# Hybrid encoder layer on one core: the first input pieces of the convolution in x landing tiles, the residual of the first tokens later, the gates of half the tokens in one store

## The chip, the cores and the metric

The kernel runs on one core of one Trainium2 chip. The metric is the device time of one execution in microseconds (us). Engines are named as the profile names them: PE (TensorE), ACT (ScalarE), DVE (VectorE), POOL (GpSimd), SP (SyncE, which issues most of the transfers); "L173" is line 173 of the kernel.

## What is computed

One encoder layer on 2048 tokens of 1024 channels, in float32. Cut to its steps:

```python
u = rms_norm(h); proj = u @ w_in
hy = short_conv_centred(proj[..., :HY_COLS])              # z, g1, g2: 512 channels each
for o, gate in enumerate((g1, g2)):                       # hyena: long convolution by rfft of 2L
    conv = irfft(rfft(z, n=2 * L) * spec[:, o], n=2 * L)[:, :L]
    z = gate * (conv + z * skip[o])
y_ml = mlstm_bidirectional(silu(short_conv(q, k)), v, o_pre, gates)   # 16 gate columns a token
h = h + concat(group_norm(z), group_norm(y_ml)) @ w_out
h = h + cross_attention(rms_norm(h), rms_norm(mem))
h = h + square(relu(rms_norm(h) @ ff_w1)) @ ff_w2
return rms_norm(h)
```

`spec` is the spectrum of two-sided filters that a small sine network makes.

## The kernel before

Every large product runs as three matmuls of split operands (high by high, low by high, high by low: L357, L360, L361 in `mm3`). All stages are Python generators that yield a cost; `weave` runs two of them side by side by these costs, so a larger `yield` puts a step later against its partner. The order that comes out is then settled by a scheduler when the program is built; `behind(ins)` (L363) tells it to place an instruction after the matmul issued last, without a semaphore.

**Input projection and filters.** `sweep` (from L749) makes channel blocks of the projection for 1024 tokens at a time, 24 matmuls for a half block of 512 tokens; DVE and ACT convolve the result (L797 to L804), and SP stores it to DRAM (`hy`, `qt`, `kt`). Woven in is `filters` (L232), which makes the filters and their transform by blocks of 32 rows against the constant `f1` (L305 to L311) and stores `fs`. Its tiles lie in the pool `f_sb` (`filters_open`, L341), which closes when it is done.

**Hyena.** `hyena` (L903) is woven with the remaining projection (`weave(rest, p.hyena(hs), 445, 329)`). Its pool `h_sb` takes the space that `f_sb` leaves. It loads `f1` again and `e2`, and then works by steps:
- `load1(j2)` (L934) loads a piece of z from `hy` with four transfers of 128 KB, in a tile of the ring "a" (ten tiles); two pieces are loaded ahead.
- `spectrum(o, j2, z)` (L990) multiplies a piece by `f1` (eight small matmuls through `beside`, L173 and L186), copies the four banks out with ACT and DVE (L997) and stores `zs`. The loop at L1004 does this for eight pieces, with a cost of 3.5 each.
- the loop at L1017 loads blocks of `fs` and `zs` (`load_block`, L915), transforms them (L955 for the filter, L1029 for z), multiplies, transforms back (L986) and stores `zg`. The first L1029 needs pieces of all eight spectra.
- the loop at L1040 loads `zg` and a gate from `hy` (`load3`), multiplies by `e2` (L173 again) and by the gate (L1050). For the first convolution each result goes into `spectrum(1, ...)`, for the second it is normed and stored as `yh`.

**Gates.** `natural` (L861) makes the token-major part of the projection; of its last column block, 16 columns are the gates of a tile of 128 tokens. They go to `sg` (two tiles in turn, L899) and to DRAM with a store per tile (L901). `gates` (L1075) reads them all and scans them on DVE (L1113, L1114).

**mLSTM and attention.** After hyena come `memproj` (L709, L738, keys and values of the memory), with steps of `mlstm` (L1283, L1199, L1321, L1323) set between them. `attention` (L1437) first turns rows of `yh` and `ym` for w_out (L1478), with casts on ACT and DVE at L368; `residual(h)` (L1505) loads half of the 512 tokens' slice of x (1 MB) into `acc`, and `finish` (L1511) adds the product to it.

The transfers of SP are issued in its program order: one whose data is not ready holds up all behind it.

## Time and profile before

| | us |
|---|---|
| median of 3 runs | 3098.77 (3090.32 to 3103.11) |
| the profiled execution | 3100.22 |
| its span in the profile | 3098.5 |
| mean granted clock of PE | 0.984 |

The span is cut in 40 slices by the page; each digit is a busy share in tenths (9 is 90% or more), the last row the mean busy share of the 16 DMA engines:

```profile
PE   9999899999999898999999999999999999999998
DVE  8855365547745445877664666557555686566695
ACT  6443356534744235565544465556555543333335
PEclk9999999999999999999999999999999999999999
DMA  6555578586767996465476556657544565354434
```

A slice is 77 us. The part that the change touches begins in the second (at 149 us, from where two loads of x move away) and ends in the sixteenth; hyena's first matmul stands at 362.67 us and its last wait of PE at 1087.53. In the timelines below, a row gives its start, its length, engine, line, operation, out<-in, and in brackets how long the engine stood idle before it and what ended that. In the rows of stretches: the window, its length, the busy time of PE with the number of instructions, the granted clock, the DMA share and GB/s.

### The profile page before, as it was taken

The page shows a single profiled execution, that of the slowest core. Times are in us where ns is not written, and L with a number is a line of the kernel's source. Part 1 is how long each engine was busy: PE and PEld are TensorE (multiplying, and loading weights), DVE is VectorE, ACT ScalarE, POOL GpSimd, SP SyncE. Part 2 cuts the span into 40 slices and gives each one's busy share as a digit, 9 for nine tenths or more (in the row PEclk, how much of TensorE's full clock was granted, in tenths as well). Part 3 has the DMA queues.
Part 4 walks back from the last instruction along what each step waited for, and adds up shares of the span by engine and source line. Part 5 has one row for each costly group of instructions (what it writes and reads, how often), then busy time and mean ns, then how long its engine had stood idle before and what let it go on. Part 6 is the DMA issues. An engine that isn't in the chain of part 4 may idle for free.

```text
span 3098.5 us, 44022 instructions
## 1 busy us (share of the span) xinstructions
PE 2989.6 (96%) x14799; PEld 2371.5 (77%) x14799; DVE 1945.6 (63%) x3442; ACT 1494.4 (48%) x2930; POOL 1121.0 (36%) x798
## 2 busy tenths in 40 slices
PE   9999899999999898999999999999999999999998
PEld 7666566776577676888888888888888888888876
DVE  8855365547745445877664666557555686566695
ACT  6443356534744235565544465556555543333335
POOL 0111012200222333333132336766466375344653
PEclk9999999999999999999999999999999999999999
DMA  6555578586767996465476556657544565354434
GB/s 223 188 191 175 198 238 250 181 268 201 241 212 217 315 303 195 152 200 167 150 245 217 188 185 226 209 179 241 196 153 151 179 213 175 110 165 119 155 102 163
DMA packets 444618, 607.06 MB, mean 196 GB/s; under 512 B 39262, under 2 KB 249054, under 8 KB 443368
## 3 DMA queue, kind: packets, MB, share of 16 engines
q1 hardware_dynamic: 407012, 546.46, 55.0%
q10 hardware_dynamic: 37380, 57.79, 5.5%
q8 instruction: 117, 1.92, 0.3%
q14 instruction: 109, 0.89, 0.1%
HBM read 401.70 MB, written 202.41 MB: 195 GB/s over the span
## 4 chain that ended last, share of the span: by engine, by line
PE 81%; DMA 9%; DVE 6%; issue 2%; ACT 1%; SPq 1%; POOL 0%; ACTq 0%; DVEq 0%; POOLq 0%
PE mm L357 17%; PE mm L361 17%; PE mm L360 17%; PE hy L357 6%; PE hy L361 6%; PE hy L360 6%; PE hy L173 2%; PE hy L1029 2%; PE hy L986 2%; PE mm L955 2%; DMA a<-zg 1%; PE mm L709 1%; PE hy L1321 1%; DMA xt<-in_x_t_dram 1%; PE hy L1323 1%
## 5 line engine op out<-in xcount | busy, mean ns | idle before, releaser
L1689 ACT CAST ah<-w 128x512 fp32r<-128x512 f32 x284 | 176.6, 623 | 302.1 <-PE hy L360 157.0
L1690 DVE TENSOR_TENSOR bl<-wr,bh 128x512 fp32r<-128x512 f32 x213 | 240.8, 1135 | 126.5 <-ACT bh L1689 126.4
L368 DVE TENSOR_TENSOR wl<-wn,wh 128x512 fp32r<-128x512 f32 (+1 forms) x296 | 215.7, 773 | 101.2 <-ACT wh L368 101.2
L357 PE MATMUL mm<-xh,wh 128*128 128x512 f32 x640 | 267.2, 419 | 3.2 <-ACT st L201 1.4
L360 PE MATMUL mm<-xl,wh 128*128 128x512 f32 x640 | 258.0, 403 | 4.5 <-DVE xl L368 4.4
L1034 POOL TENSOR_TENSOR b<-b,a 128x512 f32<-128x512 f32 x64 | 87.1, 1362 | 481.4 <-ACT b L1032 240.1
L361 PE MATMUL mm<-xh,wl 128*128 128x512 f32 x640 | 257.6, 403 | 0.0
L1689 ACT CAST bh<-wr 128x512 fp32r<-128x512 f32 x232 | 143.6, 621 | 229.9 <-PE mm L361 171.3
L1690 DVE TENSOR_TENSOR al<-w,ah 128x512 fp32r<-128x512 f32 x236 | 214.6, 910 | 55.1 <-ACT ah L1689 55.1
L361 PE MATMUL mm<-bh,al 128*128 128x512 f32 x576 | 224.1, 392 | 4.1 <-DVE al L1690 4.1
L357 PE MATMUL mm<-bh,ah 128*128 128x512 f32 x576 | 226.2, 393 | 0.5 <-DVE acc L1851 0.4
L360 PE MATMUL mm<-bl,ah 128*128 128x512 f32 x576 | 225.1, 391 | 0.0
L368 ACT CAST wh<-wn 128x512 fp32r<-128x512 f32 (+1 forms) x296 | 164.7, 620 | 105.4 <-PE mm L361 50.1
L360 PE MATMUL mm<-act,wh 128*128 128x512 f32 x512 | 201.9, 394 | 0.0
L357 PE MATMUL mm<-act,wh 128*128 128x512 f32 x512 | 199.4, 396 | 1.0 <-ACT wh L368 0.9
L361 PE MATMUL mm<-act,wl 128*128 128x512 f32 x512 | 199.6, 392 | 0.0
L357 PE MATMUL hy<-bh,ah 128*128 128x512 f32 x448 | 175.2, 391 | 0.0
L360 PE MATMUL hy<-bl,ah 128*128 128x512 f32 x448 | 174.6, 390 | 0.0
L361 PE MATMUL hy<-bh,al 128*128 128x512 f32 x448 | 174.4, 390 | 0.0
L357 PEld LDWEIGHTS mm<-xh,wh 128*128 128x128 f32 x640 | 122.4, 191 | 58.2 <-issue 24.3
L360 PEld LDWEIGHTS mm<-xl,wh 128*128 128x128 f32 x640 | 122.8, 192 | 47.4 <-issue 16.3
L357 PE MATMUL mm<-wh,xh 128*128 128x256 f32 (+1 forms) x512 | 157.4, 307 | 0.5 <-ACT st L894 0.5
(380 smaller groups left out, 8077.8 us busy)
## 6 DMA issues: line engine op xcount, KB each, us to landing
wr<-hc SPq DMA_DIRECT2D x224, 256.0 KB
w<-in_ff_w_dram SPq DMA_DIRECT2D x172, 256.0 KB
hc<-wn SPq DMA_DIRECT2D x128, 256.0 KB
wn<-in_w_in_dram SPq DMA_DIRECT2D x100, 256.0 KB
hc<-q SPq DMA_DIRECT2D x96, 256.0 KB
fs<-a SPq DMA_DIRECT2D x32, 512.0 KB
a<-fs SPq DMA_DIRECT2D x64, 256.0 KB
a<-zs SPq DMA_DIRECT2D x64, 256.0 KB
```

Source lines behind the costliest of these rows:

```text
L173: b = self.nc.tensor.matmul(*products[-1], start=True, stop=True)
L357: first = mm(ps, lh, rh, start=start, stop=False)
L360: mm(ps, lh, rl, start=False, stop=False)
L361: self.last = mm(ps, ll, rh, start=False, stop=stop)
L368: both = (self.nc.scalar.copy(hi, src), self.nc.vector.tensor_tensor(lo, src, hi.bitcast(F32), ALU.subtract))
L709: mul(p[:, m], w[:, k, ms], mt[k // 4][:, k % 4], start=k == 0, stop=k == 7)
L955: nc.tensor.matmul(pp, dm[:, m], t[:, m], start=True, stop=True)
L986: nc.tensor.matmul(pg, em[:, m], y, start=True, stop=True)
L1029: nc.tensor.matmul(pp, dm[:, m], t[:, m], start=True, stop=True)
L1034: nc.gpsimd.tensor_tensor(xt, xt, hi[:, m], ALU.mult)
L1689: self.nc.scalar.copy(hi, src)
L1690: eng.tensor_tensor(lo, src, hi.bitcast(F32), ALU.subtract)
```

## The change

Five edits:
- `f1` is one tile of the pool `i_sb`, loaded once in `filters` and used by hyena too; hyena's own load of it is gone.
- pieces 0 and 1 of `load1` go to the two tiles "xn" of `i_sb` (landing tiles of x) instead of the ring "a", which lies in space that the filters still use.
- the cost of a step of the loop over spectra is 4.2 instead of 3.5.
- the gates of eight token tiles are gathered in one tile `sg` (128 x 8 x 16), and one transfer stores them; there is one such tile.
- the load of `residual` for the first 512 tokens is placed behind the matmul issued last.

```diff
--- before.py
+++ after.py
@@ -234,7 +234,7 @@
         sd = [self.dram(f"fs{o}", (16, 64, 4, CH)) for o in range(2)]
         sb, ta, tb = self.fsb, self.ta, self.tb
         if True:
-            fw, hid, f1 = self.f_w, self.f_hid, self.f_f1
+            fw, hid, f1 = self.f_w, self.f_hid, self.f1
             nc.sync.dma_start(out=fw, in_=a["fw"])
             w1, w2, w3 = fw[0:66, 0:128], fw[:, 128:256], fw[:, 256:1280].rearrange("p (o c) -> p o c", o=2)
             par = self.par[:, 128:132]
@@ -341,10 +341,8 @@
     def filters_open(self):
         self.fes = ExitStack()
         self.fsb = self.fes.enter_context(self.tc.tile_pool(name="f_sb", bufs=1))
-        self.fsb.tile([128, 32], F32, name="f_even")
         self.f_w = self.fsb.tile([128, 1280], F32, name="fw")
         self.f_hid = self.fsb.tile([128, 16, 128], F32, name="hid")
-        self.f_f1 = self.fsb.tile([128, 128], F32, name="f1")[:, 0:64]
 
     def ta(self):
         return self.fsb.tile([128, 2, CH], F32, tag="a", name="a", bufs=7)
@@ -446,6 +444,7 @@
         self.xl = xp.tile([128, 8, 1024], F32R, name="xl")
         xp.tile([128, 56], F32, name="x_even")
         small = sb.tile([128, 448], F32, name="small")
+        self.f1 = sb.tile([128, 64], F32, name="f1")
         self.carry = small[:, 0:340].rearrange("p (c t) -> p c t", c=20)
         self.rx, self.rm = small[:, 340:356], small[:, 356:358]
         win = a["w_in"][0]
@@ -896,9 +895,12 @@
                     dst = (self.d_vd if c2 < 2 else self.d_od)[r0 - 128:r0 + 128, 256 * (c2 % 2):256 * (c2 % 2) + 256]
                     nc.scalar.dma_start(out=dst.rearrange("(t p) c -> p t c", p=128), in_=st)
                 if c2 == 3:
-                    sg = sb.tile([128, 16], F32, tag="sg", name="sg", bufs=2)
-                    nc.vector.tensor_tensor(sg, p[:, 256:272], self.gb, ALU.add)
-                    nc.sync.dma_start(out=self.d_gt[r0:r0 + 128], in_=sg)
+                    if t == 0:
+                        sg = sb.tile([128, 8, 16], F32, tag="sg", name="sg", bufs=1)
+                    nc.vector.tensor_tensor(sg[:, t], p[:, 256:272], self.gb, ALU.add)
+                    if t == 7:
+                        dst = self.d_gt[1024 * hf:1024 * hf + 1024]
+                        nc.sync.dma_start(out=dst.rearrange("(t p) g -> p t g", p=128), in_=sg)
 
     def hyena(self, es):
         nc, tc, a = self.nc, self.tc, self.a
@@ -926,13 +928,12 @@
         def tb():
             return sb.tile([128, CH], F32, tag="b", name="b", bufs=5)
 
-        f1 = sb.tile([128, 128], F32, name="f1")[:, 0:64]
+        f1 = self.f1
         e2 = sb.tile([128, 64], F32, name="e2")[:, 0:32]
-        nc.sync.dma_start(out=f1, in_=a["c_f1"])
         nc.sync.dma_start(out=e2, in_=a["c_e2"])
         ghy = self.bcast(sb, a["hy_norm_g"], CH, "ghy")
         def load1(j2):
-            z = ta()
+            z = ta() if j2 > 1 else self.isb.tile([128, D], F32, tag="xn", name="z", bufs=2).rearrange("p (j c) -> p j c", j=2)
             js = slice(2 * j2, 2 * j2 + 2)
             for q in range(4):
                 nc.sync.dma_start(out=z[phase[q]], in_=hy[0, q, :, js])
@@ -1002,7 +1003,7 @@
         yield 52
         self.strict = True
         for j2 in range(8):
-            yield 3.5
+            yield 4.2
             if j2 < 6:
                 q.append(load1(j2 + 2))
             else:
@@ -1504,7 +1505,9 @@
 
             def residual(h):
                 src = a["x_t"].rearrange("(k p) t -> p k t", p=128)[:, 4 * h:4 * h + 4, 512 * c:512 * c + 512]
-                nc.sync.dma_start(out=acc[:, 4 * h:4 * h + 4], in_=src)
+                d = nc.sync.dma_start(out=acc[:, 4 * h:4 * h + 4], in_=src)
+                if c == 0:
+                    self.behind(d)
 
             ssum = A.tile([128, 512], F32, tag="ssum", name="ssum", bufs=2)
```

What stands where, three places. First, SP near the end of the filters, before (`z` and `a<-hy` are pieces of z; `fs` and `zs` the stored transforms; `wn` weights; `f` is f1, `e` is e2; `x12` is twelve transfers):

```order
L829 DMA hy<-st 126x4x128 x2
L838 DMA qt<-cv 128x1008
L339 DMA fs_392<-a 128x1024 x2
L397 DMA wn<-in_w_in_dram 128x2x256 x4
L931 DMA f_2744<-in_c_f_dram 128x64
L932 DMA e_2745<-in_c_e_dram 128x32
L938 DMA a<-hy 32x1024 x12
L838 DMA qt<-cv 128x1008
L943 DMA dm<-in_c_dm_dram 128x256 x2
```

and now, in two stretches, the one where the first pieces stand,

```order
L828 DMA hy<-st 128x4x128 x2
L834 DMA hy<-st 16x128
L939 DMA z<-hy 32x1024 x8
L292 DMA a<-in_c_win_dram 128x1024
L339 DMA fs_390<-a 128x1024 x2
```

and the one at the end of the filters:

```order
L837 DMA qt<-cv 128x1008
L339 DMA fs_391<-a 128x1024 x2
L395 DMA wn<-in_w_in_dram 128x2x256 x4
L933 DMA e_2743<-in_c_e_dram 128x32
L939 DMA a<-hy 32x1024 x4
L944 DMA dm<-in_c_dm_dram 128x256 x2
L939 DMA a<-hy 32x1024 x3
L339 DMA zs_2736<-a 128x1024
L939 DMA a<-hy 32x1024
```

Eight of the twelve transfers moved some 35 rows up, to 213 us of the trace before, right behind the stores of what they read; the load of f1 is gone. In the same place, ACT around the first spectrum's copies (L997, now L998), before:

```order
L311 COPY a<-hy 128x512 x4
L368 CAST wh<-wn 128x512 x4
L789 COPY P<-mm 128x512
L797 ACTIVATE cv<-P,par 128x1008
L379 DMA ghy<-in_hy_norm_g_dram 128x512
L802 ACTIVATE cv<-cv 128x1008
L997 COPY a<-hy 128x512 x2
L339 DMA zs_2737<-a 128x1024
```

and now:

```order
L311 COPY a<-hy 128x512 x4
L366 CAST wh<-wn 128x512 x4
L788 COPY P<-mm 128x512
L796 ACTIVATE cv<-P,par 128x1008
L377 DMA ghy<-in_hy_norm_g_dram 128x512
L998 COPY a<-hy 128x512
L801 ACTIVATE cv<-cv 128x1008
L998 COPY a<-hy 128x512
L339 DMA zs_2736<-a 128x1024
```

One of the two copies now stands ahead of the activation of cv, and the other behind it. Second, SP ahead of the first L1029, before (`kt` is a store of convolved keys, `fs` the filter's blocks):

```order
L339 DMA zs_2737<-a 128x1024
L918 DMA a<-fs_391 128x1x512 x2
L339 DMA zs_2737<-a 128x1024 x2
L918 DMA a<-zs_2737 128x1x512 x2
L918 DMA a<-fs_391 128x1x512 x2
L918 DMA a<-zs_2737 128x1x512 x2
L838 DMA kt<-cv 128x1008
L397 DMA wn<-in_w_in_dram 128x2x256 x3
```

and now:

```order
L339 DMA zs_2736<-a 128x1024
L920 DMA a<-fs_390 128x1x512 x2
L339 DMA zs_2736<-a 128x1024
L837 DMA kt<-cv 128x1008
L395 DMA wn<-in_w_in_dram 128x2x256 x4
L339 DMA zs_2736<-a 128x1024
L837 DMA kt<-cv 128x1008
L920 DMA a<-zs_2736 128x1x512 x2
```

The loads of zs stood right behind the last two stores of zs; now two stores of kt and four loads of weights stand ahead of them too, the first store and the weights between the last two stores of zs. On PE, the fifth and the sixth spectrum stood next to each other, and 24 matmuls stand between them now; between the last spectrum and the first L1029 there were 48 matmuls and four L955, and now there are 23 and four L846. Third, SP at the start of attention, before (`acc` is the residual, `va`, `kn`, `og`, `qn`, `kk_t` and `cbn` belong to steps of mlstm):

```order
L1177 DMA kn<-kn 128x512
L1177 DMA og<-od 128x512
L1258 DMA qn<-qt 128x4x128
L1258 DMA kk_t<-kt 128x4x128
L1507 DMA acc<-in_x_t_dram 128x4x512 x2
L1258 DMA cbn<-cbd 128x516
L1183 DMA va<-vd 128x4x128
L1177 DMA kn<-kn 128x512
```

and now:

```order
L1358 DMA ym<-ht 128x512 x2
L1473 DMA wn<-ym 128x512 x2
L1184 DMA va<-vd 128x4x128
L1259 DMA cbn<-cbd 128x516
L1508 DMA acc<-in_x_t_dram 128x4x512 x2
L1178 DMA kn<-kn 128x512
L1178 DMA og<-od 128x512
L1405 DMA wn<-in_w_out_dram 128x2x256 x4
```

The two loads of the residual stood ahead of the last va; they stand behind it now, and behind the loads of the rows ym.

## The prediction

> **What bounds the kernel now.** I read the page first, then the waits of TensorE (PE), then the stretches in which they lie.

> ```profile
> span 3098.5 us, 44022 instructions
> PE 2989.6 (96%) x14799; PEld 2371.5 (77%) x14799; DVE 1945.6 (63%) x3442; ACT 1494.4 (48%) x2930; POOL 1121.0 (36%) x798
> ```

> PE is busy for 2989.6 of 3098.5 us, and the change leaves its products as they are. So a gain can only come out of the 109 us in which PE stands, and out of the slow clock that follows such a stand. The waits of PE that touch the change (us in total, times, longest):

> ```profile
> PE hy L173 <- DMA a<-hy: 11.7, 1, 11.7
> PE hy L1478 <- DVE act L368: 9.1, 1, 9.1
> PE hy L1029 <- DMA a<-zs: 7.5, 3, 4.0
> ```

> The first two are single stalls. Next, stretches of PE: window, length, busy time, granted clock, DMA share, GB/s.

> ```profile
> 755.00:975.00 220.00, 210.03 (x986) 0.99 0.67 203
> 975.00:1138.00 163.00, 146.68 (x838) 0.96 0.99 316
> 1138.00:1230.00 92.00, 80.72 (x425) 0.93 0.67 221
> ...
> 362.67:368.20 5.53, 5.53 (x25) 0.50 0.97 282
> 396.93:402.00 5.07, 5.07 (x23) 0.50 1.03 324
> 479.00:482.00 3.00, 3.00 (x8) 0.68 0.75 259
> 679.96:685.70 5.74, 5.74 (x25) 0.50 0.88 207
> 919.20:925.00 5.80, 5.73 (x27) 1.00 0.46 128
> 1202.19:1208.00 5.81, 5.80 (x24) 0.50 0.52 156
> ```

> The first three are stages; in the second the DMA engines are full (0.99). The others begin where a stall of PE ends: after the four that begin at 362.67, 396.93, 679.96 and 1202.19, PE ran 5.1 to 5.8 us at clock 0.50, so each such stall costs 2.5 to 2.9 us more than its own length.

> **The change part by part.** The order of PE is the same up to the first spectrum (PE at 351.0 in this trace) and again from about 1225 on, so all terms lie between. "Order us" below is the place of an instruction in the program, counted with these two rows, 24 matmuls of a sweep apart: 5.43 us.

> ```profile
> 415.41 0.79 PE L357 MATMUL mm<-xh,wh 128*128 128x512 f32 x1
> ...
> 420.84 0.39 PE L360 MATMUL mm<-xl,wh 128*128 128x512 f32 x1
> ```

> *1. The first pieces, issued early.* SyncE (SP) before, at two places, and what PE waited for:

> ```profile
> 213.86 0.35 SPq L292 DMA_DIRECT2D a<-in_c_win_dram  x1
> 221.27 1.30 SPq L339 DMA_DIRECT2D fs<-a  x2
> ...
> 355.64 0.34 SPq L931 DMA_DIRECT2D f<-in_c_f_dram  x1
> 356.32 0.34 SPq L932 DMA_DIRECT2D e<-in_c_e_dram  x1
> 356.72 7.84 SPq L938 DMA_DIRECT2D a<-hy  x12
> ```

> ```profile
> 362.67 1.08 PE L173 MATMUL hy<-a,f 32*64 32x512 f32 x1 [11.69 <-DMA a<-hy]
> ```

> Eight of the twelve loads now stand ahead of the c_win load at 213.86. The first spectrum has its data and its constants long before 351.0: -11.69, and -2.8 for the half of 5.53 us at half clock, so **-14.5**. The eight issues take 8 x 0.65 (7.84 / 12) = 5.2 us of SP; behind them stands the c_win load, and SP was idle for 7 us there, up to 221.27, so I take 0 (bounds 0 and +4, if the wait for the stored z comes on top). The f1 load that falls away saves 0.34 us of SP.

> What is late next? The third piece: four loads behind the wn loads, 355.64 + 0.34 + 4 x 0.65 = 358.6 at their end. Before, the first piece's four loads were out by 359.3 and let PE start at 362.67, 3.4 later; so it lands at about 362.0, needed two spectra after 351.0, at 364.0 or later. **0** (bounds 0 and +3; 1 MB of x_t now comes on SP just behind it).

> *2. The second spectrum.* It needs the banks of the first emptied. ACT empties two of them by L997, and the second of these copies now stands behind L802:

> ```profile
> 358.48 1.04 ACT L802 ACTIVATE cv<-cv 128x1008 f32<-128x1008 f32 x1 [2.64 <-DVE cv L800]
> ...
> 364.76 1.08 ACT L997 COPY a<-hy 128x512 f32<-128x512 f32 x2 [5.25 <-PE hy L186]
> ```

> So it ends at 358.48 + 1.04 + 0.54 = 360.1, and PE is there at 351.0 + 1.05 + 5.45 = 357.5: +2.6. Does a stall that short cost clock? The rows go both ways:

> ```profile
> 476.67 1.27 PE L986 MATMUL hy<-b,em 128*128 128x512 f32 x2 [2.06 <-DVE b L1035]
> ...
> 919.27 1.12 PE L986 MATMUL hy<-b,em 128*128 128x512 f32 x2 [2.44 <-DVE b L1035]
> ```

> After 2.06 idle the clock was 0.68 (row 479), after 2.44 it stayed 1.00 (row 919.20). I take half of the 2.6 us of a full spell, +1.3: **+3.9** (bounds 0 and +5.2). [...]

> *3. More sweep between spectra (yield 4.2).* Before, two spectra stood back to back, and the next waited for the copies:

> ```profile
> 396.93 1.11 PE L173 MATMUL hy<-a,f 32*64 32x512 f32 x1 [3.70 <-ACT a L997]
> ```

> Now 24 matmuls (5.43 us) stand between them: -3.70 and -2.5 of clock, **-6.2**. The price is at the other end. From the last spectrum to the first L1029, which needs its result stored and loaded again, there were 14.1 order us; now there are 6.7. How long that path is:

> ```profile
> 412.95 0.64 PE L173 MATMUL hy<-a,f 32*64 32x512 f32 x1
> ...
> 737.29 1.08 PE L173 MATMUL hy<-a,f 32*64 32x512 f32 x1 [3.89 <-issue]
> ...
> 749.15 2.39 PE L1029 MATMUL hy<-a,dm 128*128 128x512 f32 x4 [2.15 <-DMA a<-zs]
> ```

> ```profile
> 419.23 1.17 SPq L918 DMA_DIRECT2D a<-zs  x2
> ```

> At the second convolution it took 749.15 - 737.29 = 11.9 us, waited for, a good 1 us of that by half clock. At the first the loads were out at 420.4, 7.5 after the spectrum at 412.95, and landed within some 3.4: 10.9. I take 10.7 - 6.7 = 4.0 of stall and 2.5 of clock: **+6.5** (bounds 0 and 8.1). A second path gives as much: the a<-zs loads now stand on SP behind stores kt<-cv, which wait for DVE to finish a convolved half.

> For the second convolution the last two spectra now stand 2.1 apart instead of 6.0, and 7.4 order us remain before L1029 (4.5 before, with other stalls between). Against 10.7 that is 3.3 of stall where 2.15 stood: **0** (bounds -2 and +4).

> *4. Gates stored by half.*

> ```profile
> 677.21 0.17 DVE L900 TENSOR_TENSOR sg<-mm,par 128x16 f32<-128x16 f32 x1 [3.74 <-DMA gt<-sg]
> ...
> 679.96 1.11 PE L173 MATMUL hy<-a,f 32*64 32x512 f32 x1 [4.62 <-DVE a L1050]
> ```

> With two sg tiles, DVE stood 3.74 us until a store had landed, and L1050, behind it on DVE, held PE. Eight tokens' tiles now go into one buffer, whose next use is a half later, so nothing waits: -4.62 and -2.9 of clock, **-7.5**. The same bytes go out in 2 transfers for 16. But the gate scan (L1113 and L1114 on DVE), on which the stall at 737.29 above rests, has 13.4 order us of cover between L1092 and L1133 instead of 16.0: **+1.6** of the 2.6 (bounds 0 and +5).

> *5. Residual later, and a denser end of this part.*

> ```profile
> 1190.51 0.92 SPq L1507 DMA_DIRECT2D acc<-in_x_t_dram  x2
> 1192.02 0.74 SPq L1183 DMA_DIRECT2D va<-vd  x1
> ```

> ```profile
> 1230.21 0.69 DVE L1513 TENSOR_TENSOR acc<-mm,acc 128x512 f32<-128x512 f32 x1 [1.14 <-PE mm L361]
> ```

> ```profile
> 1199.66 1.28 ACT L1193 ACTIVATE ve<-va,cols 128x129 f32<-128x129 f32 x4 [4.23 <-DMA va<-vd]
> ```

> ```profile
> 1202.19 1.11 PE L1478 MATMUL hy<-ident,wn 128*128 128x128 f32 x4 [9.05 <-DVE act L368]
> ```

> The 2 MB of acc (6.3 us at 316 GB/s) go ahead of the va load; ACT waits for va at L1193, and its casts for L1478 stand behind. Now acc is issued after va, and DVE wants it only at L1513, 1230.21. So -9.05 and -2.9 go. But hyena ends 32 order us later, so the mLSTM steps before L1478 stand closer, two of them with none of the products L738 between. Such a step:

> ```profile
> 1180.59 1.06 PE L1199 MATMUL hy<-ve,kn 128*128 128x129 f32 x8
> ...
> 1189.05 1.23 PE L1199 MATMUL hy<-ve,kn 128*128 128x129 f32 x8 [0.36 <-ACT ht L1335]
> ```

> It took 8.46 us with L738 in it; bare it has 2.6 order us. Two bare ones stand for between 0 and 2 x 5.9 us; I take 6.2, the middle, and 3.2 of clock: -12.0 + 9.4 = **-2.6** (bounds -12 and +6).

> **Sum:** -14.5 + 0 + 3.9 - 6.2 + 6.5 + 0 - 7.5 + 1.6 - 2.6 = -18.8 us. The profiled execution took 3100.2 us (its span and 1.7 around it), 1.4 over the median of the three runs, 3098.8. So 3081.4 against the profile and 3080.0 against the median; I say **3081**.

> **The rivals.** Half a per cent, 15.5 us, is about what a measurement of this kernel can tell from no change.

> *The waits only move.* The stalls of terms 2, 3 and 5 come at their upper ends (5.2, 8.1 and +6, and 2 more at the second convolution): -14.5 + 5.2 - 6.2 + 8.1 + 2 - 7.5 + 1.6 + 6 = -5.3, so 3095. For it: each place where I put a new stall had little cover. Against it: all at once is much.

> *No new waits.* The prices of terms 2 and 3 vanish and the mLSTM steps cost a quarter: -14.5 - 6.2 - 7.5 + 1.6 - 12.0 + 4 = -34.6, so 3065. Against it: ACT's L802 and the 6.7 us of cover are in the order.

> *The early loads do not free PE.* The first spectrum starts on time, but its copies need a tile of the pool that opens only when the filters close, and the stores fs and the wn loads come first; then PE stands at the second or third spectrum for most of the 11.7 and its clock. The rest gives -18.8 + 14.5 = -4.3: 3096.

> *Slower: hyena's tail runs into the full stage.* Its last blocks move 32 order us later, into the stretch with DMA at 0.99. At the 203 GB/s of the stretch ahead that is 6.5 MB, 20.6 us at 316 GB/s. If the prefetched weights do not cover it, it comes as some five stalls of 4 us, each with 2.6 of clock: +33.6 in place of the -2.6, so 3100.2 - 16.2 + 33.6 = 3118. It decides from 32 us on. Against it: after 1138 the DMA share is 0.67, room to catch up, and 2 MB of acc leave the place.

> **How the numbers follow.** Forecast 0.50 (its own spread 3070 to 3092), waits only move 0.20, no new waits 0.13, early loads do not help 0.09, slower 0.08. Faster by over 0.5%, under 3083.3: 0.37 of the forecast's 0.50 and the 0.13, 0.50. Within: 0.13 + 0.20 + 0.09 = 0.42. Slower: 0.08. The range 3062 to 3103 leaves out the slower case and the far end of the no-wait case.

> **What would show it.** Right: no stall at the first L173 after the filters, clock near 1.0 there; a stall of 2 to 3 us at the second spectrum by ACT L997 and of about 4 at the first L1029; none by L1050 behind sg; the 9.05 at L1478 gone or under 3. Wrong: a stall of over 8 us by a<-hy or a<-zs between 351 and 420, or over 10 us more idle PE between 975 and 1230 than now.

## The result and the profile after

| | before | changed |
|---|---|---|
| median of 20 runs, us | 3096.61 (3090.03 to 3104.64) | 3085.94 (3078.22 to 3093.50) |
| ratio | | 0.9965 (95%: 0.9956 to 0.9975) |
| the profiled execution, us | 3100.22 | 3087.67 |
| its span | 3098.5 | 3085.6 |

The changed kernel is 10.7 us faster (0.35%; 7.7 to 13.6 by the interval of the ratio), where 17.8 (3098.8 to 3081) was forecast. The time lies inside the range; the gain is under half a per cent, to which the prediction gave a chance of 0.42, against 0.50 for more than that. The page of the changed kernel, its first lines:

```profile
span 3085.6 us, 43978 instructions
PE 2983.7 (97%) x14799; PEld 2366.8 (77%) x14799; DVE 1939.7 (63%) x3442; ACT 1492.2 (48%) x2930; POOL 1127.6 (37%) x798
```

Its waits of PE (lines of the changed kernel; most stand one or two off those of before, L1030 was L1029, L1479 was L1478):

```profile
PE hy L1030 <- DMA a<-zs: 10.8, 3, 5.2
...
PE hy L1134 <- DVE ends L1129: 5.1, 1, 5.1
...
PE hy L1479 <- DVE act L366: 4.8, 1, 4.8
PE hy L173 <- DMA a<-hy: 4.0, 1, 4.0
...
PE hy L173 <- DVE a L1051: 0.5, 1, 0.5
```

The wait of 11.7 for a<-hy is 4.0 now, the 9.1 at the turn for w_out is 4.8, and the one behind the gates' store is 0.5; the waits for zs have grown from 7.5 to 10.8, and the scan of the gates has a wait of its own. One by one, in PE's timeline:

```profile
352.19 0.64 PE L173 MATMUL hy<-z,f 32*64 32x512 f32 x1 [1.10 <-ACT a L311]
...
360.26 0.61 PE L173 MATMUL hy<-z,f 32*64 32x512 f32 x1 [1.17 <-ACT a L998]
...
384.58 0.61 PE L173 MATMUL hy<-a,f 32*64 32x512 f32 x1 [3.99 <-DMA a<-hy]
...
425.94 2.05 PE L1030 MATMUL hy<-a,dm 128*128 128x512 f32 x2 [5.16 <-DMA a<-zs]
...
719.95 0.37 PE L1134 MATMUL hy<-ident,ends 128*1 128x128 f32 x1 [5.07 <-DVE ends L1129]
...
1163.04 0.46 PE L1322 MATMUL hy<-va,rw 128*128 128x129 f32 x2 [2.29 <-DVE hy L214]
1166.53 0.80 PE L1322 MATMUL hy<-va,rw 128*128 128x129 f32 x2 [1.93 <-DVE ht L1356]
1170.74 2.09 PE L1200 MATMUL hy<-ve,kn 128*128 128x129 f32 x8 [2.12 <-ACT ht L1336]
...
1187.15 1.12 PE L1479 MATMUL hy<-ident,wn 128*128 128x128 f32 x4 [4.75 <-DVE act L366]
```

And the stretches, as before:

```profile
351.00:362.67 11.67, 9.40 (x62) 1.00 0.91 296
...
975.00:1138.00 163.00, 144.68 (x807) 0.96 0.96 306
1138.00:1230.00 92.00, 79.39 (x435) 0.91 0.65 213
```

PE ran 9.40 of the 11.67 us in which it had stood. The stall of 9.05 ended at 1202.19 in the trace of before, that of 4.75 at 1187.15 here: 15.0 us earlier. From there the work is the same and in the same order but for a few neighbouring rows, and the rest took 1896.3 us before and 1898.5 here; in the twelve other traces of this study it took 1892 to 1899. So the profiles are compared up to this point only, and the medians carry a scatter of some 3 us from behind it.

To compare stages, the loss of PE was added up from stretches of 2 us: the time not busy, plus the busy time times (1 - granted clock). Bounds are set at the same places of the program, so they shift by some us between kernels. "Cost 3.5" and "tail" are experiments told below.

| loss of PE, us | before | changed | changed, cost 3.5 (a_y35) | before, cost 4.2 (b_y42) | changed, tail earlier (a_tail) |
|---|---|---|---|---|---|
| spectra, 351 to 405 | 20.9 | 8.0 | 12.3 | 14.3 | 9.2 |
| 405 to 500 | 5.7 | 8.7 | 7.3 | 9.1 | 10.3 |
| 625 to 700 (gates' stores) | 10.4 | 1.5 | 1.8 | 3.1 | 1.2 |
| 700 to 755 (scan) | 11.9 | 14.3 | 9.4 | 11.8 | 13.1 |
| 755 to 970 | 11.4 | 7.6 | 13.5 | 12.1 | 7.0 |
| 970 to 1145 | 24.7 | 23.1 | 20.8 | 25.3 | 24.3 |
| from 1145 to the end of the slow clock behind the stall at the turn | 13.4 | 17.4 | 10.7 | 19.0 | 9.9 |

The changed kernel loses 17.8 us less than before here (98.4 less 80.6). It gained 12.9, 8.9, 3.8 and 1.6 in four stages and gave back 3.0, 2.4 and 4.0 in three.

How far one trace stands for a stage can be read from kernels that are alike up to a place. SP issues the same list up to 1190 us in the kernel before and in b_res, up to 1158 in the changed kernel and in a_nores, and up to 1053 in the changed kernel and in a_tail (the three are told below). Yet their losses in the rows ahead of 970 differ by up to 2.1 us, and in the row from 970 by up to 3.6. Up to 1145 the trace of b_res loses 5.9 us less than that of the kernel before, with the same program so far. So the 12.9 and the 8.9 stand clear of the scatter, the other gains and prices much less, and the 2.4 and the 1.6 lie inside it.

### The profile page after: what moved, and what is told of

Read it like the earlier page. It is cut to its first block, busy times and chain, and to the rows that moved or that the text cites. A ratio compares the mean times of both kernels' runs of the same rounds, so it can differ in the third digit from the quotient of the medians.

```text
span 3085.6 us, 43978 instructions
## 1 busy us (share of the span) xinstructions
PE 2983.7 (97%) x14799; PEld 2366.8 (77%) x14799; DVE 1939.7 (63%) x3442; ACT 1492.2 (48%) x2930; POOL 1127.6 (37%) x798
## 4 chain that ended last, share of the span: by engine, by line
PE 57%; DVE 2%; DMA 2%; issue 1%; ACT 1%; POOL 0%; SPq 0%; DVEq 0%; ACTq 0%; POOLq 0%
PE mm L359 12%; PE mm L355 12%; PE mm L358 12%; PE hy L359 6%; PE hy L355 6%; PE hy L358 6%; PE hy L1322 1%; PE hy L1324 1%; DMA w<-in_ff_w_dram 0%; DVE bl L1693 0%; PE hy L1596 0%; PE hy L1479 0%; PE hy L1284 0%; PE hy L1200 0%; DVE acc L1991 0%
## 5 line engine op out<-in xcount | busy, mean ns | idle before, releaser
L1035 POOL TENSOR_TENSOR b<-b,a 128x512 f32<-128x512 f32 x64 | 90.2, 1413 | 459.3 <-ACT b L1033 340.6
L358 PEld LDWEIGHTS mm<-xl,wh 128*128 128x128 f32 x640 | 120.7, 189 | 49.2 <-issue 17.8
```

The costliest lines, as they stand in the source:

```text
L358: mm(ps, lh, rl, start=False, stop=False)
L1035: nc.gpsimd.tensor_tensor(xt, xt, hi[:, m], ALU.mult)
```

## The experiments

Each part was taken out of the changed kernel, and each was put alone into the kernel before; then four kernels asked what the cost 4.2 does. All ratios are to the kernel before on the same chip (its medians there: 3097.9, 3095.1 and 3096.7). Gains in us are differences of medians; differences between two ratios are good to some 4 to 5 us.

**a_noz: changed, without the xn tiles.**

```diff
-            z = ta() if j2 > 1 else self.isb.tile([128, D], F32, tag="xn", name="z", bufs=2).rearrange("p (j c) -> p j c", j=2)
+            z = ta()
```

> The changed kernel (median 3085.9 us, first L173 after the filters at 352.19 with 1.10 of wait), with all pieces of z in the ring "a" again; f1 stays shared. Theory (the first wait is the early loads' alone): PE stands about 11 us at the first spectrum for DMA a<-hy and runs 5.5 us at half clock, +12 to +14, so 3098 to 3100. Rival (the waits only move: what stands behind it, the wait of 4.0 at 384.58 and the one of 5.2 at the first L1030, shrinks by as much as PE comes later): +5 or less, 3091 or below.

3088.42 us, ratio 0.9975 (0.9965 to 0.9984): 2.5 over the changed kernel, by the median in the rival's range. But its trace has the stall as the theory has it:

```profile
363.09 1.08 PE L173 MATMUL hy<-a,f 32*64 32x512 f32 x1 [11.99 <-DMA a<-hy]
```

The loss up to 405 is 14.7 against 8.0, and the turn is reached 5.3 us later (1192.47). With the first piece late, the fifth is no longer waited for. So 11.99 and its clock are worth 6.7 in their own stage: some of the wait only moved.

**a_y35: changed, with cost 3.5.**

```diff
-            yield 4.2
+            yield 3.5
```

> The changed kernel with the cost 3.5 again in the loop over spectra. Theory (my terms 3 and 5: the 4.2 gained 6.2 at the doubled spectrum and costs 6.5 at the first L1030, 1.6 at the gates, and most of the mLSTM stalls of 7 us ahead of L1478): faster than the changed kernel by 5 to 10, 3076 to 3081. Rival (the cost 4.2 carries a gain of its own between 633 and 975, where the loss of PE fell by 3.8 and more with no term of mine): slower by 4 or more, 3090 or above.

3073.67 us, ratio 0.9929 (0.9916 to 0.9942): 12 us faster than the changed kernel, beyond the theory's 10. What I had costed against the 4.2 is there, and the medians show more than the stages do: the turn stands 6.8 us earlier, and another 6.1 us of the trace lie in the last 1900 us, which vary by that much between traces. With 3.5 two spectra stand next to each other, and PE waits for later pieces of z instead:

```profile
384.04 1.08 PE L173 MATMUL hy<-a,f 32*64 32x512 f32 x1 [5.50 <-DMA a<-hy]
388.64 1.11 PE L173 MATMUL hy<-a,f 32*64 32x512 f32 x1 [2.47 <-ACT a L998]
```

That stage and the one from 755 lose 4.3 and 5.9 us more than with 4.2, the latter as the rival has it; the first L1030, the scan and the end lose less.

**a_sg16: changed, with a store per token tile** (two tiles sg in turn, L899 and L900 there).

```diff
-                    if t == 0:
-                        sg = sb.tile([128, 8, 16], F32, tag="sg", name="sg", bufs=1)
...
+                    sg = sb.tile([128, 16], F32, tag="sg", name="sg", bufs=2)
+                    nc.vector.tensor_tensor(sg, p[:, 256:272], self.gb, ALU.add)
+                    nc.sync.dma_start(out=self.d_gt[r0:r0 + 128], in_=sg)
```

> The changed kernel with a store of gates for each token tile, from two tiles in turn. Theory (term 4): DVE stands for a store at L900 and holds L1051 and PE for about 4.6 us, with 2.9 of clock: +6 to +8, 3092 to 3094, and the loss lies between 640 and 700. Rival (that stall came where a store happened to stand ahead of L1050 and the order has moved): within 2 us of 3086, with no stall of PE over 2 us there.

3086.95 us, ratio 0.9965 (0.9953 to 0.9978): 1 us, the rival's time. DVE waits for the stores longer than in the kernel before (18.9 us for 8.7), and PE hardly waits behind it, as the view of the tile shows (who waited for it, in turn; PEld is PE's loading of weights):

```profile
  DVE sg L899: 18.9, 4
  PEld mm L355: 1.4, 2
...
  PE mm L355: 0.2, 1
```

The stage is not as the rival has it, though: from 625 to 700 this trace loses 5.3 us, for 1.5 in the changed kernel, and PE stands over 2 us once, for a load of zg (1.21 us in the changed kernel). That the stores delay this load was not shown.

```profile
646.15 0.61 PE L173 MATMUL hy<-a,e 64*32 64x512 f32 x1 [2.40 <-DMA a<-zg]
```

**a_nores: changed, without the dependency of the residual.**

```diff
-                d = nc.sync.dma_start(out=acc[:, 4 * h:4 * h + 4], in_=src)
-                if c == 0:
-                    self.behind(d)
+                nc.sync.dma_start(out=acc[:, 4 * h:4 * h + 4], in_=src)
```

> The changed kernel without the dependency of the residual. Theory (term 5: the 2 MB hold up the va load and with it the casts for L1479): the stall at L1479, 4.75 now, grows to about 9 and its clock spell with it, +4 to +6, 3090 to 3092. Rival (the wait is that of the casts behind the mLSTM's own chain, and the load only the last to come): within 2 us of 3086.

3088.91 us, ratio 0.9973 (0.9962 to 0.9983): 3 us, between the two sides, which these runs can't tell from nothing. The stall at the turn did not grow:

```profile
1187.24 1.12 PE L1479 MATMUL hy<-ident,wn 128*128 128x128 f32 x4 [4.87 <-DVE act L366]
```

But this run does not test the theory as it was meant. Here SP issues the residual long ahead of the last va load, not just ahead of it as in the kernel before:

```profile
1158.82 0.94 SPq L1508 DMA_DIRECT2D acc<-in_x_t_dram  x2
...
1177.65 0.53 SPq L1184 DMA_DIRECT2D va<-vd  x1
```

An earlier wait grew instead, that at L1200, from 2.12 to 4.60 us, and counted as in the last row of the table the loss is 21.0 for 17.4. Whether the residual does that stays open.

**b_y42: before, with cost 4.2 alone.**

```diff
-            yield 3.5
+            yield 4.2
```

> The kernel before (3097.9 us), with the cost 4.2 for 3.5 in the loop over spectra and nothing else. Theory (4.2 costs by itself what the changed kernel gained without it, 12 us: the stall at the first L1029, the mLSTM steps without L738 ahead of L1478): slower by 8 to 13, 3106 to 3111. Rival (it costs only where the other edits have taken the waits away that cover it; alone it also moves the order so that the stall behind sg at 679.96 and the one at 396.93 go): within 4 us of 3098.

3096.31 us, ratio 0.9992 (0.9981 to 1.0004): no difference, the rival. Its trace says why: the stall of 3.70 between two spectra is gone, and of the 4.62 behind sg two small waits are left (1.59 and 0.37),

```profile
657.78 0.40 PE L357 MATMUL mm<-wh,xh 128*128 128x272 f32 x1 [1.59 <-DVE sg L900]
...
673.10 0.64 PE L173 MATMUL hy<-a,f 32*64 32x512 f32 x1 [0.37 <-DVE a L1050]
...
1180.73 0.80 PE L1321 MATMUL hy<-va,rw 128*128 128x129 f32 x2 [4.35 <-DVE ht L1355]
1185.91 2.09 PE L1199 MATMUL hy<-ve,kn 128*128 128x129 f32 x8 [3.09 <-ACT ht L1335]
```

and the steps of mlstm wait in their place; the table has 6.6 and 7.3 gained, 5.6 and 3.4 lost.

**b_early: before, with f1 shared and the two pieces in xn.** The first, second, third and fifth hunk of the change, whose last line is:

```diff
-            z = ta()
+            z = ta() if j2 > 1 else self.isb.tile([128, D], F32, tag="xn", name="z", bufs=2).rearrange("p (j c) -> p j c", j=2)
```

> The kernel before with f1 shared and the first two pieces of z in the xn tiles, and nothing else. Theory (term 1 less a wait for a later piece, as the trace of the changed kernel with cost 3.5 has it: the loss of PE from 351 to 405 was 12.3 there and 20.9 before): faster by 7 to 10, 3088 to 3091. By my term alone it would be 14.5 faster, 3083. Rival (as at cost 4.2, where taking it out cost 2.5 us): faster by 2 to 4, 3094 to 3096.

3085.34 us, ratio 0.9964 (0.9950 to 0.9978): 9.7 us by the medians, 11.1 by the ratio, as the theory has it. The loss up to 405 fell from 20.9 to 11.2; the later spectra wait:

```profile
382.75 0.61 PE L173 MATMUL hy<-a,f 32*64 32x512 f32 x1 [3.56 <-DVE P L779]
387.35 1.11 PE L173 MATMUL hy<-a,f 32*64 32x512 f32 x1 [2.73 <-ACT a L995]
```

**b_sg: before, with the gates stored by half** (and f1 shared, for room).

```diff
-                    sg = sb.tile([128, 16], F32, tag="sg", name="sg", bufs=2)
...
+                        sg = sb.tile([128, 8, 16], F32, tag="sg", name="sg", bufs=1)
```

> The kernel before with the gates stored by half, and f1 shared, which makes the room in SBUF. Theory (term 4): the stall of 4.6 behind sg at 679.96 and its clock spell go, faster by 6 to 9, 3089 to 3092. Rival (as at cost 4.2, where it was worth 1 us): within 3 us of 3098, the stall replaced by another between 640 and 700.

3088.06 us, ratio 0.9976 (0.9964 to 0.9988): 7.0 us by the medians, 7.4 by the ratio. The loss from 630 to 700 fell from 10.4 to 2.1, as the theory has it.

**b_res: before, with the residual later.**

```diff
+                if c == 0:
+                    self.behind(d)
```

> The kernel before with the residual of the first tokens behind the last matmul, and nothing else. Theory (term 5 without its denser end): the stall of 9.05 at L1478 and the clock spell after it go, faster by 9 to 12, 3086 to 3089. Rival (the va load is late for another reason, or the casts behind it wait for the mLSTM): within 3 us of 3098, a stall of over 6 us stays at L1478.

3093.35 us, ratio 0.9991 (0.9980 to 1.0002): 1.7 us by the medians, 2.8 by the ratio: the rival's time, but neither side's stall, which shrank by half.

```profile
1192.56 1.11 PE L1478 MATMUL hy<-ident,wn 128*128 128x128 f32 x4 [4.89 <-DVE act L368]
```

What stands behind it, on ACT and on DVE:

```profile
1186.32 1.28 ACT L1193 ACTIVATE ve<-va,cols 128x129 f32<-128x129 f32 x4 [1.00 <-DMA va<-vd]
...
1190.18 1.54 ACT L368 CAST act<-hy 128x512 fp32r<-128x512 f32 x3
...
1191.83 0.68 DVE L368 TENSOR_TENSOR act<-hy,act 128x512 fp32r<-128x512 f32 x1
```

The va load is in time but for 1.00 us. From L1193 at 1186.32 ACT is at work on the mLSTM step almost without a break until its casts for L1478 begin at 1190.18, 3.86 us later (in the trace of the changed kernel, where the same stretch is as long, ACT is busy for 3.82 of the 3.86 us from 1180.90 on). Of PE's 4.89 us, 2.5 go by until then and 2.4 with the casts. A stall of this size stays with the residual elsewhere, too: 4.75 us in the changed kernel, 4.87 in a_nores.

**a_m2: cost 4.2 in six steps, 1.4 in two.**

```diff
-            yield 4.2
+            yield 4.2 if j2 < 6 else 1.4
```

> The changed kernel with a cost of 4.2 in the first six steps of the loop over spectra and 1.4 in the last two, so the sum over the loop is that of 8 x 3.5 and all later steps stand as with 3.5, with no two spectra next to each other. Theory (the 12 us that 4.2 costs lie in what it pushes later: the first L1030, the gates, the mLSTM steps ahead of L1479): as fast as with 3.5 throughout (3074) or up to 4 faster, 3069 to 3075. Rival (the spacing between spectra itself costs): 3080 or above.

3082.85 us, ratio 0.9960 (0.9944 to 0.9976): the rival's range by the time, 3 us faster than the changed kernel and 9 slower than with 3.5. But the cost does not stand between the spectra, as the rival says: up to 405 the trace loses 10.5 us, for 12.3 with 3.5. The end is as with 3.5 (10.4 of loss), but two waits between are longer than there (1.64 and 4.39 us in its trace):

```profile
735.30 3.75 PE L1030 MATMUL hy<-a,dm 128*128 128x512 f32 x4 [3.73 <-DMA a<-zs]
...
1078.20 1.06 PE L173 MATMUL hy<-a,e 64*32 64x512 f32 x1 [5.80 <-DVE a L1064]
```

They and their clock are 6.6 in the two stages; what makes the rest of the 9 us was not found.

**a_tail: changed, with 3.8 for 4.5 in the last loop of hyena.**

```diff
-                yield 4.5 if o else 6.0
+                yield 3.8 if o else 6.0
```

> The changed kernel (4.2) with a cost of 3.8 for 4.5 in the last loop of hyena, 8 x 0.7 less, so that only its tail stands as with 3.5. Theory (the tail's share of the 12 us: the loss of PE from 1140 on was 17.4 in the changed kernel and 10.7 with 3.5): faster than the changed kernel by 5 to 8, 3078 to 3081, with the stalls at L1322 and L1200 of about 2 us each gone. Rival (the cost lies ahead, at the first L1030 and the gates): within 2 us of 3086.

3076.09 us, ratio 0.9938 (0.9924 to 0.9952): 9.9 us faster than the changed kernel by the medians, 8.4 by the ratios: the theory, or somewhat more. By the table its trace loses only 5.6 less. Ahead of 970 its trace loses what the changed kernel's does (40.8 and 40.1 in the first five rows of the table); at the end 9.9 for 17.4, and of the three stalls there one is left:

```profile
1172.45 1.16 PE L1200 MATMUL hy<-ve,kn 128*128 128x129 f32 x8 [2.45 <-ACT ht L1336]
...
1179.35 1.11 PE L1479 MATMUL hy<-ident,wn 128*128 128x128 f32 x4 [4.31 <-DVE act L366]
```

**a_y35noz: cost 3.5, without the xn tiles.**

```diff
-            z = ta() if j2 > 1 else self.isb.tile([128, D], F32, tag="xn", name="z", bufs=2).rearrange("p (j c) -> p j c", j=2)
+            z = ta()
...
-            yield 4.2
+            yield 3.5
```

> The changed kernel with cost 3.5 and all pieces of z in the ring "a" again (so f1, gates and residual of the change are left). Theory (at 3.5 the early loads are worth what they are alone on the kernel before, about 10 us): 3082 to 3086. Rival (as at 4.2, about 3 us): 3075 to 3078.

3086.76 us, ratio 0.9970 (0.9960 to 0.9981): 13 slower than a_y35: the theory, and 0.8 over its range. By their traces the loss up to the turn, counted from 130 us on, differs by 8.3 us (91.5 and 83.2), and at 4.2 by 8.5 (95.0 in a_noz, 86.5); by the medians it is 13 here and 2.5 there. So whether the early loads are worth less at 4.2 stays open: the traces say no, the medians yes.

**a_y30: cost 3.0.**

```diff
-            yield 4.2
+            yield 3.0
```

> The changed kernel with cost 3.0 in the loop over spectra. Theory (less is better as long as something else covers: the stall at the first L1030 and the tail shrink further, but two pairs of spectra now stand next to each other and wait for ACT's copies and for the later pieces of z): within 4 us of 3074, no gain left. Rival (it goes on as from 4.2 to 3.5, 12 us for 0.7): 3065 or below.

3073.48 us, ratio 0.9930 (0.9916 to 0.9944): no gain left against 3.5, the theory. Two pairs of spectra wait now:

```profile
371.22 0.61 PE L173 MATMUL hy<-a,f 32*64 32x512 f32 x1 [4.09 <-DVE a L998]
...
391.61 0.64 PE L173 MATMUL hy<-a,f 32*64 32x512 f32 x1 [3.75 <-ACT a L998]
```

a_y30 and a_y35 are the best kernels of this study: 3073.5 and 3073.7 us (ratios 0.9930 and 0.9929), 12 below the changed kernel and 23 to 24 below the one before.

## Why the prediction came out as it did

1. *The early loads, -14.5.* The wait went as described: PE starts its first spectrum on time, with 1.10 of wait. Mis-sized: alone on the kernel before, the edit gave 9.7. The step that failed is "what is late next? 0": I followed the third piece, which was in time, and not the fifth, for which PE now waits 3.99 with 1.7 us of slow clock behind it. SP issues the fifth piece's loads from 369.99 on, behind 1 MB of x (two transfers at 368.93); that this makes them late was not tested.

2. *The second spectrum, +3.9.* It waited for ACT's copy at L998, 1.17 us instead of 2.6. ACT was done when I had said (360.1; PE starts at 360.26), but PE came to it at 359.09 and not at 357.5. Its clock stayed whole:

```profile
360.26:366.00 5.74, 5.74 (x36) 1.00 0.74 218
```

The 1.3 of clock, half of a full spell, did not come: the granted clock was 1.00 behind these 1.17 us of idle time. Behind the 2.06 us in the trace of before it was 0.50, and behind the 2.44 it was 1.00; how the two differ is in the last section.

3. *The cost 4.2.* My own terms for it add up to -6.2 + 6.5 + 1.6 + 9.4 = 11.3 us of loss. By the medians it is 12 (a_y35 against the changed kernel), by their traces 6.8 at the turn (1180.37 and 1187.15); the stages do not show the rest. The stall at the first L1030 was 5.16 for 4.0. I did not draw the sum for this edit alone, and so did not say that the change held a part that costs as much as another brings.

4. *The gates, -7.5.* Alone, 7.0: right in size and place. But inside the change it is worth 1 by the medians (3.8 in its own stage by the traces), since 4.2 by itself takes most of the stall away (b_y42, a_sg16). My sum counted the stall under the gates and not under the 4.2, so the sum is right there; the reason why it went is shared between two edits.

5. *The residual and the end, -2.6.* This is the term that failed most. The stage from 1145 to the turn and its slow clock lost 4.0 us more, not 2.6 less. Of the 9.05 the residual held only 4.2; the other 4.9 are ACT's work on an mLSTM step and its casts (b_res). I had read the wait for va as the whole stall, because it came last. The price stood in the prediction's own row of ACT at 1199.66: ACT idled 4.23 us for va, and 9.05 - 4.23 leaves 4.8. Alone the edit gave 1.7 us by the medians, at most 6.2 by the interval of the ratio, for which I had 12.0. The denser mLSTM steps cost about what I took for them: the stalls of 2.29, 1.93, 2.12 and their clock. In a_tail, where hyena ends earlier, the first two are gone, and the last row of the table is 7.5 lower.

6. *What was not in the sum.* From 755 to 970 the loss fell by 3.8 and from 970 by 1.6 (the latter inside the scatter), waits for landing transfers and for DVE that stand otherwise in another order. In the traces, the terms that came out worse for me than forecast and the gains that I had not forecast nearly cancel: 17.8 us of loss less, for a sum of 18.8. That the two agree so well is luck, since term 5 alone was off by 6.6. The turn is 15.0 us earlier, not 17.8: about 1 us of the 17.8 is slow clock behind it, and some 2 us lie in the time that PE counts as busy, where no stall explains them. From 15.0 to the 10.7 of the medians, the rest is the profiled run of before, which lay 3.6 over its median (that of after 1.7), and the 2.1 us by which the last 1900 us ran longer.

Of the rivals, none came out whole. *The waits only move* is nearest: new or longer waits stand in most of the places that it names (5.16 and 2.85 us at L1030, 6.3 us in the mLSTM steps, but only 1.17 at the second spectrum), and 3085.9 lies between its 3095 and the forecast. *Slower* did not come: a tail that is later in the full stage lost nothing there (23.1 us after 24.7 before); it is the steps after it that were squeezed.

Of the signs named beforehand, the free start of the first spectrum, the stall at the first L1030 (5.16 for about 4) and the missing one behind sg came. The stall at the turn did not go under 3 (4.75), and that at the second spectrum stayed under 2. Neither sign of being wrong came: PE's idle time between 975 and 1230 grew by 3.3 us, not by over 10.

## What to carry to other kernels

Sum a change by edit as well as by stall: a reordering that removes two stalls for which other edits are there pays its own price for nothing, and here dropping it was worth as much as the whole change. Where a stall ends at the tail of a queue, cost only the time for which the engine of that queue idles (4.23 of 9.05 us here); what else stands in the queue stays (4.89 us in b_res). When a weave is moved, look at its far end: here the stage after it got the squeeze (17.4 us of loss for 13.4).

## What the runs showed of the hardware

```profile
385.34:388.75 3.41, 3.41 (x19) 0.50 1.02 393
422.88:429.71 6.83, 3.77 (x7) 0.50 0.83 239
719.85:726.67 6.82, 6.32 (x23) 0.50 0.61 197
1184.05:1190.88 6.83, 3.73 (x18) 0.50 0.57 188
```

Counted as in the table, PE lost half of its busy time there, 1.7, 1.9, 3.2 and 1.9 us, not always the 2.5 to 2.9 that the prediction took from the trace of before. In rows of half a us, all 24 changes of the clock between 340 and 1240 us in the trace of before, and all 20 in that of the changed kernel, lay within 0.02 us of one grid of 3.413 us in each trace. On this grid the two stalls which the prediction could not tell apart differ: the 2.06 us at 476.67 lie in one step, the 2.44 at 919.27 in two, 1.00 us in the first and 1.44 in the second. The clock was 0.50 in the step behind the one, and 1.00 in both steps of the other and behind it (919.20 to 925.00).

```profile
474.10:477.51 3.41, 1.35 (x7) 1.00 0.62 186
477.51:480.92 3.41, 3.41 (x7) 0.50 0.94 301
...
914.42:917.83 3.41, 2.41 (x21) 1.00 0.79 231
917.83:921.24 3.41, 1.97 (x6) 1.00 0.72 224
```

The 0.68 that the prediction read behind the 2.06 is the mean of a row (479 to 482) that lies across the end of the slow step at 480.92. Between 341 and 1238 us in the trace of before, the clock fell behind every step at full clock in which PE was idle for 1.97 us or more, and behind none with 1.61 or less; between 372 and 1235 in the changed kernel, the least idle time behind which it fell was 1.81, and the most behind which it did not was 1.89. So in these two traces the idle time within one step told the cases apart except between 1.81 and 1.89 us; no run varied it by itself.

The last 1900 us, from the stall at the turn on, the same instructions in nearly the same order, took 1892 to 1899 us from trace to trace.
